# Plain float32 products in four column groups for the first modulation, and the first products in feature order

## The chip, the cores and the metric

The kernel runs on one core of a Trainium2 chip. The metric is the device time of one execution in microseconds. Engines are named as in the profile: PE is TensorE (PEld its weight loads), DVE VectorE, ACT ScalarE, POOL GpSimd, SP the engine whose queue issues nearly all DMA transfers.

## The reference

One layer of a diffusion backbone: 1024 latent tokens and 256 context tokens of width 1024. The part at issue is its start: a conditioning vector gives shifts and scales (a vector-matrix product with `w_mod`), these modulate an RMS norm, and the result goes through the input projection.

```python
sc, scc = jax.nn.silu(c), jax.nn.silu(c_ctx)
m_lat = sc @ w_mod[l] + b_mod[l]
m_ctx = scc @ w_mod[l] + b_mod[l]
sh1, sc1, g1, sh2, sc2, g2 = [t[:, None, :] for t in jnp.split(m_lat, N_MOD, axis=-1)]
csh1, csc1, cg1, csh2, csc2, cg2 = jnp.split(m_ctx, N_MOD, axis=-1)

h_lat = rms_norm(x, norm1_g[l]) * (1.0 + sc1) + sh1
h_ctx = rms_norm(ctx, norm1_g[l]) * (1.0 + csc1) + csh1
...
split_heads(h_lat @ w_in, rope_r, rope_d)
split_heads(h_ctx @ w_in, None, None)
...
k_all = jnp.concatenate([dk_c, dk_l], axis=3)
```

Retention, differential attention, output projection, gated residual, a second modulated norm, a gated MLP with a depthwise convolution, and a final norm follow; the change touches none of them.

## The kernel before

Everything is in float32. A large product is made of three passes over operands split into a high and a low float32r part (helper `passes`, L129 to L132: high x high, high x low, low x high), each a 128 x 128 weight block against up to 512 columns. Plain float32 products are used in a few places.

**Start of the kernel.** Four blocks of `w_mod`, 512 columns wide (1024 x 512, the order of the blocks is scale and shift of features 0 to 511, then scale and shift of features 512 to 1023), are loaded as 16 tiles `wt` of 512 KB, two blocks of 128 rows each. `modulation1(half)` does two of the blocks. For each 128-row block the silu of the two conditioning vectors (`csil`, 128 x 2) is the weight of a matmul and the `wt` rows stream past: into `pr`, one PSUM bank. The string table `GEMV` says which of the 32 row blocks go as a plain float32 product (L506, "1", 21 of them) and which as a split one (L511 to L514, "0", 11 of them): ACT makes `mhi`, DVE makes `mlo`, and two float32r matmuls with `csplit` (4 columns: high and low part of both vectors) take them. At the end of a block ACT copies `pr` to `rw`, and four short products with `fold` (L520), called a fold below, add the parts up and turn the row into columns `mcol`, to which DVE adds the bias. So there are four folds, two in each half.

**Beside it.** `raw_latents` loads the first four tiles `xt` of 128 tokens, normalizes them (ACT squares, DVE, POOL's power step, DVE multiplies, L529 to L531) and turns them with PE transposes `px` into `xraw` (features on partitions). `xt` and `wt` share one ring of five 512 KB buffers, so each transfer waits until the one five places ahead is used up. After the second fold `first_latents(0)` modulates features 0 to 511 (L582 on DVE, high part L583 on ACT, low part L585 on DVE or POOL) and does their part of the products for the attention's keys: heads `h` outside, feature blocks `k` inside, three passes each into `pl`. It is called by `tick` from inside the modulation's loop, so its steps stand between the weight products of the second half. The w_in slices `raw` that these products need are split into `whi` and `wlo` by `split_slice` (L180 to L184). After the fourth fold comes the rest: features 512 to 1023 of the same products and `rotated` (rotary step and store), with `context_rows` beside it (two tiles `xc`, turned and modulated into `cT`), then the products `pc` of the context, with the second four token tiles (`latents`) beside them, then `pl` of the second token half, 96 products, then the value projection `pn`.

**What sets the order.** The program order is written by hand with `beside` and `tick`. A scheduler then lists the instructions per engine by its own cost model and buffer counts; each engine runs its list in order. Each transfer of SP's queue waits in line too.

## Time and profile before

| | |
|---|---|
| median of 3 runs | 1462.45 us (1458.42 to 1463.15) |
| profiled execution | 1465.94 us, its span 1464.2 us |
| mean granted TensorE clock | 0.990 |
| PE busy in 0 to 32 us | 24.13 us |
| DVE busy in 60 to 80 us | 19.04 us |
| `wt` transfers | 16 of 512 KB, median 4.4 us from issue to landing |

The span runs from the first to the last instruction. Times in the views are from the span's start. A timeline row gives the start, the time from the first start to the last end of the merged instructions, the engine, the line, the names and the count, and in brackets the idle time before it and what ended that. Matmuls are pipelined: a record's length is more than the step to the next one.

### The profile page before, as it was taken

The page shows a single profiled execution, that of the slowest core. Times are in us where ns is not written, and L with a number is a line of the kernel's source. Part 1 is how long each engine was busy: PE and PEld are TensorE (multiplying, and loading weights), DVE is VectorE, ACT ScalarE, POOL GpSimd, SP SyncE. Part 2 cuts the span into 40 slices and gives each one's busy share as a digit, 9 for nine tenths or more (in the row PEclk, how much of TensorE's full clock was granted, in tenths as well). Part 3 has the DMA queues.
Part 4 walks back from the last instruction along what each step waited for, and adds up shares of the span by engine and source line. Part 5 has one row for each costly group of instructions (what it writes and reads, how often), then busy time and mean ns, then how long its engine had stood idle before and what let it go on. Part 6 is the DMA issues. An engine that isn't in the chain of part 4 may idle for free.

```text
span 1464.2 us, 19441 instructions
## 1 busy us (share of the span) xinstructions
PE 1399.3 (96%) x6924; PEld 1145.3 (78%) x6924; DVE 1008.7 (69%) x1491; ACT 739.6 (51%) x1409; POOL 362.7 (25%) x466
## 2 busy tenths in 40 slices
PE   7999999999899899889999989999999999999996
PEld 2587888787778789779888767888888888888885
DVE  4687355333577599778334889777787787998457
ACT  4665212322456688778423654555544545555433
POOL 1320000021788324651001253222322220000001
PEclk9999999999999999999999999999999999999999
DMA  8548755465455757561322123222332234963324
GB/s 289 204 169 274 241 180 174 142 188 180 140 168 174 192 126 183 137 119 30 141 104 87 43 94 123 93 96 106 108 109 104 98 108 148 387 220 115 101 94 173
DMA packets 107753, 218.30 MB, mean 149 GB/s; under 512 B 8964, under 2 KB 47364, under 8 KB 106760
## 3 DMA queue, kind: packets, MB, share of 16 engines
q1 hardware_dynamic: 99592, 192.41, 38.6%
q0 software_dynamic: 8064, 24.64, 7.4%
q8 instruction: 55, 0.90, 0.3%
q14 instruction: 42, 0.34, 0.1%
HBM read 159.61 MB, written 57.41 MB: 148 GB/s over the span
## 4 chain that ended last, share of the span: by engine, by line
PE 69%; DVE 8%; DMA 6%; ACT 4%; POOL 3%; issue 3%; SPq 0%; POOLq 0%; DVEq 0%; ACTq 0%
PE chain L130 5%; PE chain L131 5%; PE chain L132 5%; PE pv L774 4%; PE pA L742 4%; PE c L132 3%; PE c L131 3%; PE c L130 3%; PE pn L130 3%; PE pn L132 3%; PE pn L131 3%; PE third L130 2%; DMA W<-w_down 2%; PE third L132 2%; PE third L131 2%
## 5 line engine op out<-in xcount | busy, mean ns | idle before, releaser
L130 PE MATMUL pl<-hT,whi 128*128 128x512 f32 x256 | 107.6, 422 | 0.7 <-ACT hT L583 0.7
L130 PE MATMUL chain<-T,whi 128*128 128x512 f32 x264 | 103.5, 392 | 3.1 <-ACT ub L1120 1.3
L131 PE MATMUL pl<-hT,whi 128*128 128x512 f32 x256 | 101.8, 398 | 1.6 <-DVE hT L585 1.3
L131 PE MATMUL chain<-T,whi 128*128 128x512 f32 x264 | 102.9, 390 | 0.0
L132 PE MATMUL chain<-T,wlo 128*128 128x512 f32 x264 | 102.3, 390 | 0.4 <-DVE wlo L909 0.4
L132 PE MATMUL pl<-hT,wlo 128*128 128x512 f32 x256 | 101.0, 395 | 0.5 <-DVE wlo L184 0.5
L742 PE MATMUL pA<-ks,qhl 128*128 128x512 f32 (+1 forms) x384 | 94.3, 383 | 4.5 <-ACT p L749 4.5
L745 DVE TENSOR_REDUCE mt<-pA 128x1 f32<-128x1280 f32 x64 | 95.1, 1488 | 3.7 <-PE pA L742 2.3
L1036 POOL TENSOR_TENSOR cmb<-wrb 128x512 f32<-128x512 f32 x22 | 35.3, 1603 | 247.8 <-DMA wrb<-w_up 138.6
L132 PE MATMUL c<-whi,ghl 128*128 128x512 f32 x232 | 90.4, 390 | 0.3 <-DVE ghl L1195 0.3
L130 PE MATMUL c<-whi,ghl 128*128 128x512 f32 x232 | 90.3, 389 | 0.0
L131 PE MATMUL c<-wlo,ghl 128*128 128x512 f32 x232 | 90.3, 389 | 0.0
L749 ACT ACTIVATE p<-pA,mt 128x1280 f32<-128x1280 f32 x64 | 85.3, 1332 | 5.0 <-DVE mt L745 4.9
L116 POOL TENSOR_TENSOR sm<-sm,mhalf 128x1 f32<-128x1 f32 x26 | 16.7, 640 | 283.1 <-DVE sm L115 277.2
L742 PEld LDWEIGHTS pA<-ks,qhl 128*128 128x128 f32 x384 | 71.0, 198 | 17.7 <-ACT p L749 5.5
L908 ACT CAST whi<-cmb 128x512 fp32r<-128x512 f32 x66 | 41.0, 622 | 83.2 <-PE chain L131 61.2
L909 DVE TENSOR_TENSOR wlo<-cmb,whi 128x512 fp32r<-128x512 f32 x66 | 63.7, 968 | 23.4 <-ACT whi L908 23.3
L774 PE MATMUL pv<-va,aT 128*128 128x128 f32 x640 | 77.8, 277 | 0.5 <-DVE yT L803 0.2
L130 PE MATMUL pn<-whi,hT 128*128 128x512 f32 x192 | 77.8, 405 | 0.0
L774 PEld LDWEIGHTS pv<-va,aT 128*128 128x128 f32 x640 | 73.9, 192 | 2.7 <-DVE yT L803 1.9
L132 PE MATMUL pn<-whi,hT 128*128 128x512 f32 x192 | 75.4, 393 | 0.0
L131 PE MATMUL pn<-wlo,hT 128*128 128x512 f32 x192 | 75.1, 391 | 0.0
(309 smaller groups left out, 3934.1 us busy)
## 6 DMA issues: line engine op xcount, KB each, us to landing
wm<-w_mod SPq DMA_DIRECT2D x32, 512.0 KB, 4.5
raw<-w_in SPq DMA_DIRECT2D x28, 512.0 KB, 4.5
wra<-w_up SPq DMA_DIRECT2D x24, 512.0 KB, 3.3
wrb<-w_up SPq DMA_DIRECT2D x24, 512.0 KB, 3.4
W<-w_down SPq DMA_DIRECT2D x44, 256.0 KB, 6.2
ad<-s SPq DMA_DIRECT2D x20, 512.0 KB, 3.3
wra<-ad SPq DMA_DIRECT2D x20, 512.0 KB, 3.3
wrb<-ad SPq DMA_DIRECT2D x18, 512.0 KB, 3.4
```

Of the source, the lines that this page charges most:

```text
L116: nc.gpsimd.tensor_tensor(out=out_ap, in0=out_ap, in1=mhalf[:, :n], op=ALU.pow)
L130: mm(ps, lh, rh, start=first, stop=False, skip_group_check=more)
L131: mm(ps, lh, rl, start=False, stop=False, skip_group_check=more)
L132: mm(ps, ll, rh, start=False, stop=last, skip_group_check=more)
L742: mm(self.pa[m][:, c0:c1], self.q[:, i, m, qs], self.k[:, m, c0:c1], start=(i == 0), stop=(i == 1))
L745: nc.vector.tensor_reduce(out=self.mt[:, m : m + 1], in_=self.pa[m][:, :LK], axis=AX.X, op=ALU.min)
L749: nc.scalar.activation(self.p[m], self.pa[m][:, :LK], AF.Exp, scale=-1.0, bias=self.mt[:, m : m + 1], accum_out=self.s[:, m : m + 1])
L774: mm(self.pv, self.aT[:, c, :], self.v[:, c, :], start=(c == 0), stop=(c == NKT - 1))
L908: nc.scalar.copy(hi, src)
L909: nc.vector.tensor_tensor(out=lo, in0=src, in1=r32(hi), op=ALU.subtract)
L1036: nc.gpsimd.tensor_tensor(out=s1, in0=b1, in1=b2, op=ALU.add)
```

## The change

The table `GEMV` and the split path are gone: all 32 row blocks go as plain float32 products. `cz` holds the two conditioning columns with 30 zero columns behind them for each row block (a POOL memset and a DVE copy). Four row blocks at a time, each with its own 32 columns as weights, write the partitions 0 to 31, 32 to 63, 64 to 95 and 96 to 127 of `pr`; a second group of four adds to them. `fold` is now 128 x 2 and adds up the four groups. `rw` is 128 rows high instead of 4.

The order around it changes too. The loads of the four `x` tiles are issued from inside the modulation, one before every second `wt` tile; a token tile is turned one step later than it is normalized; the two w_in slices that were loaded in the first half come behind all of its loads. The products of features 0 to 511 run in feature order: block `k` outside, the four heads inside, with all four `pl` banks open. The rest of the features runs heads 0 and 1 together in feature order, then head 2, then head 3.

```diff
--- before.py
+++ after.py
@@ -58,7 +58,6 @@
 R_LAM = R_DEC + 8
 
 
-GEMV = ("01111111", "00111111", "01010101", "01010101")
 TAIL = 2
 EARLY = ("S1", "M1", "S0", "M0", "E1", "E0", "R", "C")
 OPS = dict(S="scores", M="least", E="exp", R="ratio", C="combine", T="turn", K="turned", V="values", O="out", Q="square", f="rstd", n="norm", Y="final", h="high", l="low")
@@ -485,36 +484,34 @@
 
         with ExitStack() as p0:
             xp = p0.enter_context(tc.tile_pool(name="xp", bufs=1))
-            csplit = xp.tile([P, KD, 4], F32R, name="csplit")
-            nc.vector.tensor_copy(csplit[:, :, 0:2], csil)
-            nc.vector.tensor_tensor(out=csplit[:, :, 2:4], in0=csil, in1=r32(csplit[:, :, 0:2]), op=ALU.subtract)
-            fold = xp.tile([4, 2], F32, name="fold")
-            nc.vector.tensor_tensor(out=fold, in0=ident[:4, 0:2], in1=ident[:4, 2:4], op=ALU.add)
-            bsc = xp.tile([P, KD], F32, name="bsc", bufs=3)
+            cz = xp.tile([P, KD, 32], F32, name="cz")
+            nc.gpsimd.memset(cz, 0.0)
+            nc.vector.tensor_copy(cz[:, :, 0:2], csil)
+            fold = xp.tile([P, 2], F32, name="fold")
+            nc.vector.tensor_tensor(out=fold, in0=ident[:, 0:2], in1=ident[:, 32:34], op=ALU.add)
+            for g in (64, 96):
+                nc.vector.tensor_tensor(out=fold, in0=fold, in1=ident[:, g : g + 2], op=ALU.add)
+            bsc = xp.tile([P, KD], F32, name="bsc", bufs=7)
             nc.vector.tensor_scalar(out=bsc, in0=cl[:, COL_BMOD + 8 : COL_BMOD + 16], scalar1=1.0, scalar2=None, op0=ALU.add)
 
-            def modulation1(half):
+            def modulation1(half, between, beyond):
+
                 d0 = 4 * half
                 for i in range(2 * half, 2 * half + 2):
                     s = 1 - i % 2
                     pr = mm_tile("pr")
-                    for kk in range(KD // 2):
-                        raw = xp.tile([P, 2, 512], F32, name="wt", tag="xt", bufs=5)
-                        nc.sync.dma_start(out=raw, in_=w_mod[i][:, 2 * kk : 2 * kk + 2, :])
-                        for j in range(2):
-                            if GEMV[i][2 * kk + j] == "1":
-                                mm(pr[:2, :], csil[:, 2 * kk + j, :], raw[:, j, :], start=False, stop=(kk + j == KD // 2))
-                                tick()
-                                continue
-                            whi = xp.tile([P, 512], F32R, name="mhi", bufs=2)
-                            wlo = xp.tile([P, 512], F32R, name="mlo", bufs=2)
-                            nc.scalar.copy(whi, raw[:, j, :])
-                            nc.vector.tensor_tensor(out=wlo, in0=raw[:, j, :], in1=r32(whi), op=ALU.subtract)
-                            mm(pr[:4, :], csplit[:, 2 * kk + j, :], whi, start=(kk + j == 0), stop=False)
-                            mm(pr[:4, :], csplit[:, 2 * kk + j, :], wlo, start=False, stop=(kk + j == KD // 2))
-                            tick()
-                    rw = xp.tile([4, 512], F32, name="rw", bufs=2)
-                    nc.scalar.copy(rw, pr[:4, :])
+                    for q in range(2):
+                        raw = []
+                        for kk in (2 * q, 2 * q + 1):
+                            raw.append(xp.tile([P, 2, 512], F32, name="wt", tag="xt", bufs=5))
+                            nc.sync.dma_start(out=raw[-1], in_=w_mod[i][:, 2 * kk : 2 * kk + 2, :])
+                            if kk % 2 == 0:
+                                next(between, None)
+                        for g in range(4):
+                            mm(pr[32 * g : 32 * g + 32, :], cz[:, 4 * q + g, :], raw[g // 2][:, g % 2, :], start=(q == 0), stop=(q == 1))
+                        next(beyond, None)
+                    rw = xp.tile([P, 512], F32, name="rw", bufs=2)
+                    nc.scalar.copy(rw, pr)
                     pm = pst.tile([P, 4, 2], F32, name="pm", tag="tr")
                     for j in range(4):
                         mm(pm[:, j, :], rw[:, j * P : (j + 1) * P], fold, start=True, stop=True)
@@ -558,39 +555,61 @@
             wget, more = stream_parts(5)
             part = []
 
+            xs0 = []
+
+            def row_loads():
+                for t in range(4):
+                    xs0.append(xp.tile([P, D], F32, name="xt", tag="xt", bufs=5))
+                    nc.sync.dma_start(out=xs0[t], in_=x[t * P : (t + 1) * P, :])
+                    yield
+
+            def turn_raw(t):
+                for g in range(2):
+                    pt = pst.tile([P, 4, P], F32, name="px", tag="tr")
+                    for i in range(4):
+                        d = 4 * g + i
+                        nc.tensor.transpose(pt[:, i, :], xs0[t][:, d * P : (d + 1) * P], ident)
+                    dst = xraw[:, 4 * g : 4 * g + 4, t * P : (t + 1) * P]
+                    if g == 0:
+                        nc.scalar.copy(dst, pt)
+                    else:
+                        nc.vector.tensor_copy(dst, pt)
+
             def raw_latents():
                 for t in range(4):
-                    xt = xp.tile([P, D], F32, name="xt", tag="xt", bufs=5)
-                    nc.sync.dma_start(out=xt, in_=x[t * P : (t + 1) * P, :])
+                    normalize(xs0[t], 2 + t)
+                    if t:
+                        turn_raw(t - 1)
                     yield
-                    normalize(xt, 2 + t)
-                    for g in range(2):
-                        yield
-                        pt = pst.tile([P, 4, P], F32, name="px", tag="tr")
-                        for i in range(4):
-                            d = 4 * g + i
-                            nc.tensor.transpose(pt[:, i, :], xt[:, d * P : (d + 1) * P], ident)
-                        dst = xraw[:, 4 * g : 4 * g + 4, t * P : (t + 1) * P]
-                        if g == 0:
-                            nc.scalar.copy(dst, pt)
-                        else:
-                            nc.vector.tensor_copy(dst, pt)
-
-            def first_latents(half):
-                for d in range(4 * half, 4 * half + 4):
-                    hi, lo, raw = hT[0][0][:, d, :], hT[1][0][:, d, :], xraw[:, d, :]
-                    nc.vector.tensor_scalar(out=raw, in0=raw, scalar1=mcol[:, d, 1, 0:1], scalar2=mcol[:, d, 0, 0:1], op0=ALU.mult, op1=ALU.add)
-                    nc.scalar.copy(hi, raw)
-                    eng = nc.gpsimd if d % 2 else nc.vector
-                    eng.tensor_tensor(out=lo, in0=raw, in1=r32(hi), op=ALU.subtract)
+
+            def modulated(d):
+                hi, lo, raw = hT[0][0][:, d, :], hT[1][0][:, d, :], xraw[:, d, :]
+                nc.vector.tensor_scalar(out=raw, in0=raw, scalar1=mcol[:, d, 1, 0:1], scalar2=mcol[:, d, 0, 0:1], op0=ALU.mult, op1=ALU.add)
+                nc.scalar.copy(hi, raw)
+                eng = nc.gpsimd if d % 2 else nc.vector
+                eng.tensor_tensor(out=lo, in0=raw, in1=r32(hi), op=ALU.subtract)
+
+            def part_products(h, k):
+                passes(part[h], wget(k, h * P, (h + 1) * P), tuple(hT[a][0][:, k, :] for a in range(2)), k == 0, k == KD - 1)
+
+            def first_half():
+                part.extend(mm_tile("pl") for _ in range(H))
+                for k in range(4):
+                    modulated(k)
+                for k in range(4):
+                    for h in range(H):
+                        part_products(h, k)
                     yield
-                for h in range(H):
-                    if half == 0:
-                        part.append(mm_tile("pl"))
-                    for k in range(4 * half, 4 * half + 4):
-                        passes(part[h], wget(k, h * P, (h + 1) * P), tuple(hT[a][0][:, k, :] for a in range(2)), k == 0, k == KD - 1)
-                        yield
-                    if half == 1:
+
+            def second_half():
+                for k in range(4, KD):
+                    modulated(k)
+                for hs in ((0, 1), (2,), (3,)):
+                    for k in range(4, KD):
+                        for h in hs:
+                            part_products(h, k)
+                            yield
+                    for h in hs:
                         rotated(part[h], dk_d, rtab, 32, 1.0, LC, h, 0)
 
             def context_rows():
@@ -608,19 +627,16 @@
                     modulate(xc, d, 1, cT[0][:, d, :], cT[1][:, d, :])
                     yield
 
-            beside(raw_latents(), 0.75, 1.0)
-            modulation1(0)
+            modulation1(0, row_loads(), raw_latents())
+            turn_raw(3)
             more()
             more()
-            beside(first_latents(0), 1.25, 0.0)
-            modulation1(1)
-            beside(iter(()), 0.0)
+            modulation1(1, iter(()), first_half())
             more()
             more()
             rtab = load_rope(1)
-            todo = first_latents(1)
-            for _ in range(4):
-                next(todo)
+            todo = second_half()
+            next(todo)
             beside(context_rows(), 0.75, 0.0)
             for _ in todo:
                 tick()
```

Three places of the built order show what this moves. First PE from the start of the modulation to the second fold; `pr` are the weight products, `px` the turns of the token tiles, `pm` a fold. Before:

```order
L513 MATMUL pr<-mhi,csplit 4x512
L514 MATMUL pr<-mlo,csplit 4x512
L506 MATMUL pr<-wt,csil 2x512 x2
L572 MATMUL px<-ident,xt 128x128 x4
L506 MATMUL pr<-wt,csil 2x512
L572 MATMUL px<-ident,xt 128x128 x4
L506 MATMUL pr<-wt,csil 2x512 x3
L572 MATMUL px<-ident,xt 128x128 x4
L506 MATMUL pr<-wt,csil 2x512
L572 MATMUL px<-ident,xt 128x128 x4
L520 MATMUL pm<-fold,rw 128x2 x4
```

Now:

```order
L511 MATMUL pr<-wt,cz 32x512 x4
L571 MATMUL px<-ident,xt 128x128 x8
L511 MATMUL pr<-wt,cz 32x512 x4
L517 MATMUL pm<-fold,rw 128x2 x4
L571 MATMUL px<-ident,xt 128x128 x7
L511 MATMUL pr<-wt,cz 32x512 x2
L571 MATMUL px<-ident,xt 128x128
L511 MATMUL pr<-wt,cz 32x512 x2
L571 MATMUL px<-ident,xt 128x128 x8
L511 MATMUL pr<-wt,cz 32x512 x4
L517 MATMUL pm<-fold,rw 128x2 x4
L571 MATMUL px<-ident,xt 128x128 x8
```

The first list ends at the first fold, the second at the turns of the last token tile, behind the second fold: the weight products stand in runs of two tiles, and the turns of a token tile are no longer spread between them.

SP's queue over the same stretch. Before:

```order
L503 DMA wt<-w_mod 128x1024
L564 DMA xt<-x 128x1024
L503 DMA wt<-w_mod 128x1024
L564 DMA xt<-x 128x1024
L503 DMA wt<-w_mod 128x1024 x2
L180 DMA raw<-w_in 128x1024
L564 DMA xt<-x 128x1024
L503 DMA wt<-w_mod 128x1024 x2
L564 DMA xt<-x 128x1024
L503 DMA wt<-w_mod 128x1024 x2
L180 DMA raw<-w_in 128x1024
L503 DMA wt<-w_mod 128x1024 x8
```

Now:

```order
L507 DMA wt<-w_mod 128x1024
L563 DMA xt<-x 128x1024
L507 DMA wt<-w_mod 128x1024 x2
L563 DMA xt<-x 128x1024
L507 DMA wt<-w_mod 128x1024 x2
L563 DMA xt<-x 128x1024
L507 DMA wt<-w_mod 128x1024 x2
L563 DMA xt<-x 128x1024
L507 DMA wt<-w_mod 128x1024
L179 DMA raw<-w_in 128x1024 x2
L507 DMA wt<-w_mod 128x1024 x8
```

The two w_in slices have moved behind the last transfer of the first half; a token tile now comes with every two weight tiles.

DVE around the fourth fold, which ends in the row `mcol<-pm,cl`; `xc` are the context tiles. Before:

```order
L184 TENSOR_TENSOR wlo<-raw,whi 128x1024 x2
L512 TENSOR_TENSOR mlo<-wt,mhi 128x512
L115 TENSOR_SCALAR sm<-sm 128x1
L531 TENSOR_SCALAR xc_540<-xc_540,sm 128x1024
L115 TENSOR_SCALAR sm<-sm 128x1
L531 TENSOR_SCALAR xc_550<-xc_550,sm 128x1024
L523 TENSOR_TENSOR mcol<-pm,cl 128x4x2
L115 TENSOR_SCALAR sm<-sm 128x1
L582 TENSOR_SCALAR xraw<-xraw,mcol 128x512 x4
L585 TENSOR_TENSOR hT_170<-xraw,hT_168 128x512
```

Now:

```order
L183 TENSOR_TENSOR wlo<-raw,whi 128x1024
L520 TENSOR_TENSOR mcol<-pm,cl 128x4x2
L587 TENSOR_SCALAR xraw<-xraw,mcol 128x512
L183 TENSOR_TENSOR wlo<-raw,whi 128x1024
L590 TENSOR_TENSOR hT_170<-xraw,hT_168 128x512
L587 TENSOR_SCALAR xraw<-xraw,mcol 128x512 x3
L590 TENSOR_TENSOR hT_170<-xraw,hT_168 128x512
L114 TENSOR_SCALAR sm<-sm 128x1
L528 TENSOR_SCALAR xc_490<-xc_490,sm 128x1024
L114 TENSOR_SCALAR sm<-sm 128x1
L528 TENSOR_SCALAR xc_500<-xc_500,sm 128x1024
```

The context tiles are normalized behind the modulation of the second four feature blocks, where they stood ahead of the fourth fold, and one of two splits of a w_in slice has moved behind the fold.

## The prediction

> **What bounds the kernel now.** I read the page first (busy shares, then the 40 slices), then the table of stretches, then the timeline of the first 130 us. The built order of every engine differs only there and in a few places up to about 180 us; behind that it is the same instruction for instruction.
>
> ```profile
> PE 1399.3 (96%) x6924; PEld 1145.3 (78%) x6924; DVE 1008.7 (69%) x1491; ACT 739.6 (51%) x1409; POOL 362.7 (25%) x466
> ...
> sum 32.00, PE 24.13 PEld 7.92 DVE 12.13 ACT 14.16 POOL 2.39; mean PE 1.51 PEld 0.49 DVE 0.76 ACT 0.89 POOL 0.15
> ...
> 20.00:25.00 5.00, 4.71 (x14) 1.55 (x14) 1.65 (x6) 1.74 (x3) 0.55 (x1) 0.66 0.86 302
> ...
> 60.00:65.00 5.00, 3.36 (x11) 1.89 (x12) 4.77 (x6) 2.81 (x7) 3.70 (x3) 1.00 0.00 0
> 65.00:70.00 5.00, 5.00 (x24) 4.03 (x24) 4.53 (x9) 4.89 (x10) 1.74 (x3) 1.00 0.01 3
> 70.00:80.00 10.00, 9.36 (x62) 7.89 (x61) 9.74 (x19) 9.71 (x18) 2.99 (x3) 1.00 0.19 73
> ```
>
> TensorE is busy 96% of the span, so a microsecond taken off it early moves everything behind. In a row of the table the columns are PE, PEld, DVE, ACT, POOL, then the clock. TensorE is also what the first 32 us wait for (24.13 busy, and nearly all of its idle time is before the first weights arrive), then up to 58 us. From 60 to 80 us VectorE is full (4.77, 4.53 and 9.74, 19.04 of 20 us) and TensorE has holes. So there are three stages with different limits: first half of the modulation (to the second fold), second half (to the fourth fold), and a tail that VectorE sets.
>
> ```profile
> 5.85 0.62 ACT L511 CAST mhi<-wt 128x512 fp32r<-128x512 f32 x1 [2.83 <-DMA wt<-w_mod]
> 7.10 1.06 ACT L529 ACTIVATE sq<-xt 128x1024 bf16<-128x1024 f32 x1 [0.63 <-DMA xt<-x]
> 7.77 3.25 PE L506 MATMUL pr<-wt,csil 128*2 128x512 f32 x4
> 8.58 0.13 PEld L506 LDWEIGHTS pr<-wt,csil 128*2 128x2 f32 x1 [0.72 <-DMA wt<-w_mod]
> 9.68 1.06 ACT L529 ACTIVATE sq<-xt 128x1024 bf16<-128x1024 f32 x1 [1.43 <-DMA xt<-x]
> 13.08 2.74 PE L506 MATMUL pr<-wt,csil 128*2 128x512 f32 x6
> 28.20 0.66 PE L572 MATMUL px<-ident,xt 128*128 128x128 f32 x4
> 29.84 0.58 ACT L517 COPY rw<-pr 4x512 f32<-4x512 f32 x1 [0.36 <-PE pr L506]
> 30.47 1.05 PE L520 MATMUL pm<-fold,rw 4*128 4x2 f32 x8
> 31.45 0.40 PE L513 MATMUL pr<-mhi,csplit 128*4 128x512 f32 x1
> ...
> L506 PE MATMUL pr<-wt,csil x42: 591/592/1061, 7.8 to 55.4; 128*2 128x512 f32 x42
> ...
> wt<-w_mod SPq DMA_DIRECT2D x16, 512.0 KB, 4.4
> ```
>
> A plain float32 product is two records (x42 for 21 products). Six take 2.74 us and the last is 0.592 long, so the pitch is (2.74 - 0.59)/5 = 0.43 us, 0.86 for a product. Early ones ran at nearly twice that (four in 3.25). The second fold ends at 31.45, the fourth, below, at 58.50.
>
> **The change, part by part.** It removes 21 plain products, 11 split ones (22 short matmuls, with 11 copies on ACT and 11 subtractions on DVE) and adds 32 plain products, four to a group, each in its own 32 columns. DVE and ACT were not the limit before 58 us, so their savings there count for nothing; what counts is the price of a group on TensorE.
>
> That price no row shows: nothing in this trace runs in another column group. Bounds from the 0.43 pitch: the records of a pair one after the other, 4 x 0.43 = 1.72; both products wholly at once, 2 x 0.43 = 0.86. Between them: the low record of one product must follow its own high record, but the next product's high record can run beside it, 3 x 0.43 = 1.29 (five pitches, 2.15, for four). I take this middle, since matmuls here start in program order, and keep both ends. [...]
>
> *First half.* Here the loads set the pace. The first five 512 KB transfers (five buffers) land at 5.85, 7.10, 8.58, 9.68 and, by the same step of 1.25, about 11.0. The new order takes w0 w1, turns x0, takes w2 w3, folds, turns x1, takes w4 w5, turns x2, takes w6 w7, folds, turns x3. The w0 w1 products at the slow early pitch end about 10.5; eight turns (2 x 0.66) 11.8; w2 and w3 (asked for when w0 is free, about 8.7, landed by 12.9) 14.1; copy 0.58 and fold 1.05 to 15.8; turns of x1 to 17.1. Only that frees the buffer of w6. The queue is in order, so w6 lands some 4 us later at 21.2 (median 4.4), x3 at 22.4, w7 at 23.7; their products to 25.0, copy and fold to 26.6. So the second fold ends 31.45 - 26.6 = 4.9 earlier. Serial products make it 28.8 (2.7 earlier), wholly parallel ones 26.0 (5.5 earlier). TensorE now waits on loads from 18 to 23, and where it paused before, the granted clock fell (0.66 in 20 to 25); a repeat would cost up to 2 of this.
>
> *Second half.*
>
> ```profile
> 30.43 0.69 DVE L577 COPY xraw<-px 128x512 f32<-128x512 f32 x1 [1.59 <-PE px L572]
> 32.25 1.00 DVE L582 TENSOR_SCALAR xraw<-xraw,mcol 128x512 f32<-128x512 f32 x2
> 32.88 1.14 ACT L583 CAST hT<-xraw 128x512 fp32r<-128x512 f32 x2 [1.42 <-DVE xraw L582]
> 50.04 0.40 PE L130 MATMUL pl<-hT,whi 128*128 128x512 f32 x1
> 50.27 0.39 PE L131 MATMUL pl<-hT,whi 128*128 128x512 f32 x1
> 54.99 1.02 PE L506 MATMUL pr<-wt,csil 128*2 128x512 f32 x2
> 55.94 0.50 PE L130 MATMUL pl<-hT,whi 128*128 128x512 f32 x1
> 57.52 1.05 PE L520 MATMUL pm<-fold,rw 4*128 4x2 f32 x8
> 58.50 0.64 PEld L537 LDWEIGHTS pt<-ident,xc 128*128 128x128 f32 x6
> ```
>
> Before, 58.50 - 31.45 = 27.05. A feature product has a pitch of 0.23; entering and leaving a plain product costs 55.94 - 54.99 - 0.86 = 0.09. Now: the eight turns of x3 (1.32), the copy (0.69), the modulation of one feature block (0.50) and its high part (0.57) come first, 3.1; then 48 feature products x 0.23 = 11.0, six pairs of weight products x 1.38 = 8.3, one run of four 2.24, two folds x 0.98 = 2.0. Sum 26.6, a gain of 0.4. Serial: eight x 1.81 = 14.5 in place of 10.5, 30.6, a loss of 3.6. Parallel: seven entries x 0.95 = 6.7, 22.8, a gain of 4.3. The w_in slices, which now queue behind all the first half's loads, land about 26, before their use at 28.
>
> Fourth fold: 4.9 + 0.4 = 5.3 earlier; serial 0.9 later, parallel 9.8 earlier.
>
> *Tail.*
>
> ```profile
> 60.61 3.55 POOL L585 TENSOR_TENSOR hT<-xraw,hT 128x512 fp32r<-128x512 f32 x2 [0.76 <-ACT hT L583]
> 65.44 0.75 DVE L531 TENSOR_SCALAR xt<-xt,sm 128x1024 f32<-128x1024 f32 x1 [0.66 <-POOL sm L116]
> 92.61 0.40 PE L130 MATMUL pl<-hT,whi 128*128 128x512 f32 x1
> 95.52 0.68 DVE L544 TENSOR_TENSOR hT<-tmp,hT 128x512 fp32r<-128x512 f32 x1
> 115.00:120.00 5.00, 3.02 (x13) 1.87 (x12) 5.00 (x7) 4.56 (x8) 0.00 (x0) 1.00 0.82 273
> 120.00:125.00 5.00, 3.82 (x17) 2.83 (x16) 4.55 (x6) 1.20 (x2) 0.00 (x0) 1.00 1.00 344
> 126.01 1.22 DVE L184 TENSOR_TENSOR wlo<-raw,whi 128x1024 fp32r<-128x1024 f32 x1
> ...
> PE pn L131 <- DVE wlo L184: 1.9, 1, 1.9
> ```
>
> Both context tiles were normalized before the fourth fold. Now that stands behind the second features' modulation on DVE, and its power step behind POOL's low parts, 3.55 for two; one wlo split (1.22) also slips behind the fold, another moves ahead of the second token half. That is 2 x (0.75 + 0.15) + 2 x 1.22 = 4.2 more on the engine that is full there, and a wait for POOL. Walking the new order with these durations, the last low part on DVE comes 45 after the fourth fold, where it was at 96.2 - 58.5 = 37.7. TensorE can do 33 of the 96 products of the second token half by then and ends them 59.8 after the fold, not 92.61 + 96 x 0.23 - 58.5 = 56.3: 3.4 lost. But it then runs into a wait it has already: 1.98 + 1.18 = 3.2 idle from 115 to 125, until the fourth split of the value weights, done 127.2 - 58.5 = 68.7 after the fold. In the new order I get 66.8, because VectorE's idle gaps behind 96 us are used up. The wait that ends last decides: between 1.9 gained and, if it is gone, 3.4 lost. I take 1.0 gained.
>
> *Sum:* 4.9 + 0.4 + 1.0 = 6.3 us. The profiled execution took 1465.94 (span 1464.2), 3.5 above the median of the runs, so 1459.6 against it and 1462.45 - 6.3 = 1456.2 against the median.
>
> **Rivals.**
>
> *Columns wholly at once.* 9.8 + 1.0 = 10.8 gained, 1451.7. For: four groups have four destinations and the source lays them next to each other. Against: each product is two records that need the same columns. [...]
>
> *Columns one after another.* 0.9 lost, 1.0 gained in the tail: 1462.3, no change. For: every plain record in this trace follows the one before at a full pitch. Against: all those share their columns, so they had to.
>
> *Every step between column groups exposes a weight load.* This is the other side. Place: second half, where nothing covers TensorE.
>
> ```profile
> 11.54 0.09 PEld L506 LDWEIGHTS pr<-wt,csil 128*2 128x2 f32 x2 [0.17 <-issue]
> 13.51 0.08 PEld L506 LDWEIGHTS pr<-wt,csil 128*2 128x2 f32 x1 [0.34 <-issue]
> ```
>
> Price: on top of serial products, the 0.17 seen where kinds change, on 32 records, 5.4, and about 1 more in the first half: 0.9 + 5.4 + 1.0 - 1.0 = 6.3 lost, 1468.8. It decides (slower by over 0.3%) from about 0.12 a record. Against: the load at 13.51 ran inside the matmul before. [...]
>
> *The tail's lag goes through.* 45 - 37.7 = 7.3 lost instead of 1.0 gained: 5.3 - 7.3 = 2.0 slower, 1464.5. For: VectorE is full from 60 to 80. Against: TensorE has 33 products and all context products to do meanwhile.
>
> **How the numbers follow.** About 0.3% (4.4 us) is what a measurement of this kernel can tell from no change. The forecast (partial overlap) has 0.38: of it 0.28 faster, 0.09 within, 0.01 slower; own range 1452 to 1460. Wholly parallel 0.22, all faster. Serial 0.18: 0.03 faster, 0.11 within, 0.04 slower. Exposed loads 0.13, slower. Tail 0.09: 0.03, 0.04, 0.02. Together 0.56, 0.24 and 0.20. The range runs from 1449 (past the parallel case) to 1467 (short of exposed loads).
>
> **What would show it.** The starts of the eight records of a group: steps of 0, 0.43, 0, 0.43 between products mean partial overlap, all within 0.86 parallel, eight even steps serial; wider ones exposed loads. The second fold should end near 26.6 and the fourth near 53.2. In the tail, the last low part of the second token half some 45 after that, and a TensorE wait before the value products that ends about 67 after it. A second fold later than 29, or a group that takes over 3.4, makes the forecast wrong.

## The result, and the profile after

The changed kernel took 1463.25 us (median of 22 runs, 1459.24 to 1469.08), the kernel before 1462.37 us beside it (22 runs, 1458.42 to 1467.4). The ratio is 1.0002, with a 95% interval from 0.999 to 1.0014: no change that can be told. Forecast were 1456.2 us and, as the likeliest, faster.

The profiled execution of the changed kernel has a span of 1458.7 us, 5.5 below that of the kernel before. That difference is not the change. The last value product on context tiles (behind the work that the change touches) starts at 244.15 us, before at 243.49; the 5.5 us arise later, in work that both kernels share. There the trace of the kernel before has four more stretches at half the clock than that of the changed one (from about 260, 365, 510 and 600 us), each worth 1.7 us of clock. The table of stretches shows the first of them. First the kernel before, then the changed one; the number ahead of the last two is the granted clock:

```profile
255.00:260.00 5.00, 2.52 (x9) 1.43 (x9) 4.59 (x6) 0.98 (x2) 0.00 (x0) 0.97 0.42 157
260.00:265.00 5.00, 5.00 (x17) 3.37 (x16) 0.69 (x1) 1.76 (x3) 0.00 (x0) 0.68 0.50 184
```

```profile
255.00:260.00 5.00, 3.32 (x12) 1.99 (x11) 4.58 (x7) 1.29 (x3) 0.00 (x0) 1.00 0.42 151
260.00:265.00 5.00, 5.00 (x26) 3.97 (x25) 0.56 (x1) 1.55 (x3) 0.00 (x0) 1.00 0.51 185
```

A hole here is a time in which TensorE stands. Both traces have one (5 - 2.52 = 2.5 us and 5 - 3.32 = 1.7); one was followed by a stretch at half the clock (17 matmuls in 5 us instead of 26), the other was not. So a single trace says little of the whole time here, and I compare milestones of the first 250 us.

The same table of the changed kernel for the first 90 us (PE, PEld, DVE, ACT, POOL, then the clock):

```profile
15.00:20.00 5.00, 2.99 (x16) 0.92 (x15) 1.78 (x5) 1.74 (x3) 0.55 (x1) 1.00 0.90 335
20.00:25.00 5.00, 3.06 (x17) 1.08 (x17) 1.60 (x3) 2.32 (x4) 0.55 (x1) 1.00 1.01 382
25.00:30.00 5.00, 3.11 (x17) 2.71 (x17) 2.09 (x4) 2.27 (x4) 0.00 (x0) 0.57 1.01 385
30.00:35.00 5.00, 5.00 (x12) 1.85 (x14) 4.71 (x7) 2.48 (x4) 1.72 (x2) 0.50 0.43 137
35.00:40.00 5.00, 5.00 (x19) 1.99 (x18) 0.15 (x1) 0.00 (x0) 1.27 (x1) 0.91 0.51 164
55.00:60.00 5.00, 4.76 (x13) 3.64 (x14) 4.20 (x7) 3.39 (x7) 2.54 (x2) 0.66 0.51 178
80.00:90.00 10.00, 6.97 (x50) 5.53 (x49) 8.07 (x15) 6.72 (x12) 3.42 (x4) 1.00 0.45 159
```

TensorE now has holes from 15 to 30 us (it waits for the modulation's weights, for the copies of its own results and for the token tiles), and the clock is at half from 25 to 35 us and again between 56 and 60. The clock lost is (0.43 + 0.50 + 0.09) x 5 = 5.1 us, and 0.34 x 5 = 1.7 more; the kernel before had one such stretch here, 1.7 us. (This counts clock, not time: where TensorE stands anyway, a low clock costs nothing.) From 80 to 90 us TensorE stands 3 of 10 us. The timeline of TensorE shows what the low clock does, and the price of the column groups (L511 their products, L571 the turns, L517 the folds, L129 to L131 the products of the first features):

```profile
24.97 1.26 PE L517 MATMUL pm<-fold,rw 128*128 128x2 f32 x8 [0.69 <-ACT rw L514]
26.09 1.95 PE L571 MATMUL px<-ident,xt 128*128 128x128 f32 x8
31.07 1.92 PE L511 MATMUL pr<-wt,cz 128*32 128x512 f32 x4
...
45.25 1.05 PE L511 MATMUL pr<-wt,cz 128*32 128x512 f32 x4
46.23 0.50 PE L130 MATMUL pl<-hT,whi 128*128 128x512 f32 x1
...
48.95 1.07 PE L511 MATMUL pr<-wt,cz 128*32 128x512 f32 x8
49.94 0.50 PE L129 MATMUL pl<-hT,whi 128*128 128x512 f32 x1
52.80 0.95 PE L517 MATMUL pm<-fold,rw 128*128 128x2 f32 x8
55.24 0.97 PE L129 MATMUL pl<-hT,whi 128*128 128x512 f32 x3 [1.49 <-ACT hT L588]
```

A pair of products takes 46.23 - 45.25 = 0.98 us, four take 49.94 - 48.95 = 0.99: the columns run wholly at once. A pair takes 1.92 at half clock. (The pair at 8.21 us takes 1.92 too, where the clock column reads 1.00; what slows it there is not shown.) The second fold ends at 26.2 and the fourth at 53.75, 4.75 us earlier than before.

The tail is the work from the fourth fold to the first value product on latents (`pn` from `hT`). First two rows and a stretch of the kernel before:

```profile
68.75 1.06 ACT L529 ACTIVATE sq<-xt 128x1024 bf16<-128x1024 f32 x1
127.09 0.39 PE L130 MATMUL pn<-whi,hT 128*128 128x512 f32 x1
...
80.00:90.00 10.00, 9.26 (x73) 8.35 (x71) 8.85 (x15) 8.22 (x13) 2.40 (x2) 1.00 0.40 152
```

The changed kernel, in rows of ScalarE, VectorE and TensorE and of TensorE's waits:

```profile
65.42 4.82 ACT L420 ACTIVATE xb<-pl 32x512 f32<-32x512 f32 x8
82.38 1.05 ACT L526 ACTIVATE sq<-xt 128x1024 bf16<-128x1024 f32 x1
87.06 0.55 PE L534 MATMUL pt<-ident,xt 128*128 128x128 f32 x3 [1.32 <-DVE xt L528]
99.62 0.68 DVE L541 TENSOR_TENSOR hT<-tmp,hT 128x512 fp32r<-128x512 f32 x1
116.15 0.39 PE L131 MATMUL pl<-hT,wlo 128*128 128x512 f32 x1
123.78 1.21 DVE L183 TENSOR_TENSOR wlo<-raw,whi 128x1024 fp32r<-128x1024 f32 x1
128.57 0.39 PE L129 MATMUL pn<-whi,hT 128*128 128x512 f32 x1
...
PE pt L534 <- DVE xt L528: 2.2, 2, 1.3
```

The first value product on latents starts at 128.57 us, 74.8 after the fourth fold, where it was 127.09 - 58.50 = 68.6: 6.2 us lost, against 4.75 gained ahead of it.

### The profile page after: what moved, and what is told of

Same layout as the page of the kernel before. It is cut to its first block, busy times and chain, and to the rows that moved or that the text cites. A ratio compares the mean times of both kernels' runs of the same rounds, so it can differ in the third digit from the quotient of the medians.

```text
span 1458.7 us, 19406 instructions
## 1 busy us (share of the span) xinstructions
PE 1388.4 (95%) x6924; PEld 1142.0 (78%) x6924; DVE 995.8 (68%) x1481; ACT 732.6 (50%) x1398; POOL 360.6 (25%) x467
## 4 chain that ended last, share of the span: by engine, by line
PE 69%; DVE 10%; DMA 8%; ACT 5%; POOL 4%; issue 4%; SPq 0%; POOLq 0%; ACTq 0%; DVEq 0%
PE chain L129 5%; PE chain L130 5%; PE chain L131 5%; PE pv L790 4%; PE c L131 3%; PE c L129 3%; PE c L130 3%; PE pA L758 3%; PE pn L130 3%; PE pn L131 3%; PE pn L129 3%; PE third L129 2%; PE third L130 2%; PE third L131 2%; PE po L131 2%
## 5 line engine op out<-in xcount | busy, mean ns | idle before, releaser
L129 PE MATMUL pl<-hT,whi 128*128 128x512 f32 x256 | 108.1, 426 | 4.0 <-ACT hT L588 3.4
L129 PE MATMUL chain<-T,whi 128*128 128x512 f32 x264 | 103.5, 392 | 3.0 <-ACT ub L1136 1.3
L131 PE MATMUL chain<-T,wlo 128*128 128x512 f32 x264 | 102.4, 390 | 0.4 <-DVE wlo L925 0.4
L131 PE MATMUL pl<-hT,wlo 128*128 128x512 f32 x256 | 102.0, 399 | 0.0
L131 PE MATMUL c<-whi,ghl 128*128 128x512 f32 x232 | 90.4, 389 | 0.5 <-DVE ghl L1211 0.5
L129 PE MATMUL c<-whi,ghl 128*128 128x512 f32 x232 | 90.3, 389 | 0.0
L129 PE MATMUL pn<-whi,hT 128*128 128x512 f32 x192 | 78.2, 407 | 0.0
L131 PE MATMUL pn<-whi,hT 128*128 128x512 f32 x192 | 75.0, 391 | 0.0
```

The lines of the kernel that those rows point to most:

```text
L129: mm(ps, lh, rh, start=first, stop=False, skip_group_check=more)
L131: mm(ps, ll, rh, start=False, stop=last, skip_group_check=more)
```

## The experiments

Three theories of where the gain went were tried. **Clock**: the faster columns leave TensorE waiting, the granted clock halves behind such holes, and that takes the gain. **Tail**: two heads now end together, their rotation copies fill ScalarE (65.42, 4.82 us), the normalizations of the second token half come late (squares to 83.4 us, before to 70), and TensorE has holes from 80 to 101 us. **Order**: computing the first features' products in feature order is what costs. A table of all runs first. Clock is the mean over the timed runs of each kernel (in brackets: one run). The last three columns, in us, are from one trace each: end of the fourth fold, start of the first value product on latents, start of the last value product on context tiles. A filler is a product whose result nothing reads.

| kernel | ratio to before (95%) | clock | fold | latents | context |
|---|---|---|---|---|---|
| before | 1 | 0.991 | 58.5 | 127.1 | 243.5 |
| changed | 1.0002 (0.999 to 1.0014) | 0.987 | 53.8 | 128.6 | 244.2 |
| e5, changed again | one run | (0.990) | 53.0 | 127.7 | 242.7 |
| e1, early normalization | 1.0007 (0.9992 to 1.0022) | 0.9865 | 54.5 | 129.1 | 247.1 |
| e2, head order | 1.0016 (1.0005 to 1.0027) | 0.985 | 52.0 | 127.1 | 243.4 |
| e3, 48 fillers | 0.9964 (0.9949 to 0.9978) | 0.9915 | 52.8 | 126.3 | 242.2 |
| e4, one column set | one run | (0.991) | 59.6 | 128.0 | 242.6 |
| e6, 25 fillers | 0.9969 (0.9955 to 0.9983) | 0.992 | 48.1 | 121.7 | 237.6 |
| e7, fillers, head order | 0.999 (0.9977 to 1.0003) | 0.991 | 49.3 | 122.4 | 238.6 |
| e8, e7 with early norm. | 0.9998 (0.9981 to 1.0014) | 0.991 | 48.1 | 121.2 | 238.2 |
| e9, e6, early norm., own raw | 0.9984 (0.9966 to 1.0001) | 0.991 | 49.9 | 119.9 | 241.7 |
| e10, e6, own raw | 0.9982 (0.997 to 0.9994) | 0.991 | 48.6 | 121.5 | 240.5 |
| e11, 19 fillers | one run | (0.991) | 48.1 | 121.6 | 237.5 |
| e12, before with 3 fillers | one run | (0.991) | 58.0 | 126.0 | 244.2 |

**Four products through one set of columns (e4).**

```
-mm(pr[32 * g : 32 * g + 32, :], ..., start=(q == 0), stop=(q == 1))
+mm(pr[:32, :], ..., start=(q + g == 0), stop=(q + g == 4))
```

> The changed kernel with all four weight tiles of a run put through the same 32 columns, added up in one place, so that nothing can run side by side; same count of products, fold over 32 rows instead of 128. If the groups of the changed kernel run wholly at once (run of four 0.99 us, one alone 0.86): a run of four takes 3.3 to 3.5 us here, second fold later by 1 to 4 us (loads cover part), fourth fold later by 9 to 12 us than 53.75, span 5 to 12 us longer. If the columns gave nothing and the pace came from elsewhere: a run of four stays below 1.5 us and the folds within 1 us.

From its timeline and its table of stretches:

```profile
52.09 3.62 PE L509 MATMUL pr<-wt,cz 128*32 128x512 f32 x8
58.58 1.05 PE L515 MATMUL pm<-fold,rw 32*128 32x2 f32 x8
...
20.00:25.00 5.00, 3.56 (x20) 1.79 (x19) 2.64 (x4) 2.81 (x6) 0.55 (x1) 1.00 1.02 389
25.00:30.00 5.00, 4.33 (x14) 1.19 (x12) 2.18 (x4) 2.58 (x4) 0.55 (x1) 1.00 0.88 274
```

Four products in one place take 3.62 us, beside each other 1.07 in the same measure: 3.4 times. But the fourth fold is only 5.9 us later than in the changed kernel (9 to 12 expected), and nothing runs at half speed: the clock is 1.00 up to 260 us. And at 128 us the two kernels stand together (128.0 against 128.6). The comparison at full clock is with e6 below, the changed kernel with its holes filled: there the fold is 59.6 - 48.1 = 11.5 us earlier than here, as expected, the first value product on latents 6.3, the last on context tiles 5.0. The eight weight loads of a run of four are 0.109 us each (median of the changed kernel), 0.87 us one after another; in the run at 48.95 us of the changed kernel they lie within 0.16 us at its start, so they run beside each other too.

**Fillers for the clock (e3, e6, e11).** They are products of the ones tile with itself, 128x128, and each run of them stands behind a chosen product (the lines that fix its place are not shown):

```
+def warm(n):
+    wm = pst.tile([P, P], F32, name="wm", tag="tr")
+    ...
+    for _ in range(n):
+        mm(wm, ones, ones, start=True, stop=True)
 for g in range(4):
+    if i == 1 and g == 2:
+        warm(4 if q == 0 else 5)
     mm(pr[32 * g : 32 * g + 32, :], ...)
 turn_raw(3)
+warm(8)
```

These lines are of e6, which has 2 more ahead of the second fold and 6 behind the fourth; e11 leaves the 6 out. In e3 they stand in runs of 8, 8, 8, 12 and 12.

> The changed kernel with short products of the ones tile (128x128, results never read) put into the waits of TensorE: eight behind each of three quarters of the first half, twelve ahead of the second half's columns, twelve behind the fourth fold. They compute nothing that is used. Clock theory: the granted clock stays near 1.0 from 25 to 35 us (0.57 and 0.50 in the changed kernel), the stretch from the first features' products to the second pair of columns takes 3.4 instead of 6.4 us, and the fourth fold ends at 49.5 to 51.5 instead of 53.75. If loads bind instead: clock near 1.0 but the fold within 1 us of 53.75. If the clock follows something other than the idle of TensorE: 0.5 to 0.6 stays. For the whole time: tail theory says that an earlier fold is lost again behind late normalizations, ratio 0.999 to 1.001; if the tail passes it on, 0.997 to 0.998.

The clock stayed up but for one stretch at 27 to 30 us (mean of the timed runs 0.9915, changed kernel 0.987), and the time fell by 0.36%, more than expected for an earlier fold. The fillers were too many: they pushed the second fold from 26.2 to 31.8 us, and the fourth, at 52.8, missed its forecast (49.5 to 51.5) but still came 0.95 earlier than in the changed kernel. At the last value product on context tiles only 243.5 - 242.2 = 1.3 us are gained on the kernel before; where the rest of the 0.36% arises is not shown.

> The changed kernel with 25 short products of the ones tile (results never read) fitted into the holes of TensorE that its trace shows: 4 and 5 between the two products of the third and fourth runs of the first half, 2 ahead of the second fold, 8 behind the last turns, 6 behind the fourth fold; in all 6.0 us of work at 0.24 us each (from the run with 48 of them), 6.7 us of holes. Clock theory: no half-speed period ahead of 60 us (6.8 us lost in the changed kernel), second fold at 25 to 26.5, fourth fold at 48.5 to 50.5 instead of 53.75, time 1456 to 1459, ratio 0.996 to 0.998, spread of the runs smaller. If only the tail's order counts: fold earlier, last value product on context tiles still at 243 to 244.5, ratio 0.999 to 1.001.

Its timeline and table:

```profile
21.05 1.05 PE L522 MATMUL pr<-wt,cz 128*32 128x512 f32 x4 [0.25 <-DMA wt<-w_mod]
22.03 1.38 PE L501 MATMUL wm<-ones 128*128 128x128 f32 x10
26.11 0.95 PE L530 MATMUL pm<-fold,rw 128*128 128x2 f32 x8
47.17 0.95 PE L530 MATMUL pm<-fold,rw 128*128 128x2 f32 x8
121.72 0.39 PE L129 MATMUL pn<-whi,hT 128*128 128x512 f32 x1
...
25.00:30.00 5.00, 5.00 (x48) 4.75 (x50) 3.51 (x6) 3.46 (x5) 0.00 (x0) 1.00 0.99 385
30.00:35.00 5.00, 4.16 (x24) 2.33 (x20) 4.41 (x7) 2.29 (x4) 1.82 (x2) 1.00 0.86 304
55.00:60.00 5.00, 4.90 (x25) 3.76 (x26) 3.03 (x8) 2.99 (x6) 1.89 (x3) 1.00 0.05 20
```

The second fold ends at 27.1 (25 to 26.5 forecast), 0.8 later than in the changed kernel, the clock is 1.00 up to 60 us, and the fourth fold ends at 48.1 us, 5.6 earlier. All of it is still there at 122 us (121.7 against 128.6) and at 238. The time is 1457.09 us, median of 7 runs, against 1463.12 beside it (25 runs). Its ratio lies, like that of e3, below those of both kernels with intervals apart, by work that computes nothing.

> The changed kernel with the 19 short products of the first half and last turns, and without the 6 behind the fourth fold. Clock theory: no half-speed period from 25 to 35 us, fourth fold at 47.5 to 48.5 (53.75 in the changed kernel), then one period of half speed begins within 5 us of the fold's end (1.5 us of hole there, as in both traces of the changed kernel), and first value product on latents at 122.5 to 124, that is 1 to 2 us behind the run with all 25. If the six are worthless: within 0.5 us of 121.7.

No half-speed stretch followed the hole behind the fourth fold here (1.49 us), and the six were worth nothing in this trace (121.6 us): the second branch. So the same hole is followed by half speed in both traces of the changed kernel and not in this one. The traces together say more than one of them. The four with columns and without fillers (changed, e5, e1, e2) have three or more half-speed stretches from 20 to 60 us each; the six with the fitted fillers (e6 to e11) have none there.

**A second trace of the changed kernel (e5).**

> The changed kernel itself, nothing edited, for a second trace. Clock theory (runs of the changed kernel hold a mean granted clock of 0.987 against 0.991 of the kernel before, though the one trace at hand has 0.991; the clock is lost in whole periods of 3.4 us at half speed that follow a period with holes on TensorE, and which periods are hit differs from run to run): the half-speed periods ahead of 60 us come again, and this trace shows 1 to 4 further ones, above all between 80 and 130 us, where the first trace has holes. Tail theory alone: the same periods as in the first trace, the same span within 1 us.

```profile
20.00:25.00 5.00, 4.48 (x18) 2.09 (x20) 1.00 (x3) 1.63 (x3) 0.40 (x1) 0.66 0.97 334
30.00:35.00 5.00, 4.73 (x14) 1.79 (x14) 4.71 (x7) 2.83 (x5) 1.30 (x2) 0.66 0.76 279
55.00:60.00 5.00, 5.00 (x16) 3.79 (x15) 3.39 (x6) 3.98 (x8) 3.35 (x3) 0.66 0.38 135
```

Three stretches ahead of 60 us, 5.1 us of clock, at other places than in the first trace; none between 80 and 130 us, where I expected more. (Such ones do come in the traces of e2, at 85 to 95 us, and e1, at 120.)

**The tail (e1, e2).** In e1 the loads and normalizations of xc and of x4 to x7 are called right behind the second half's modulation; in e2 both halves take the products head by head.

```
 next(todo)
+rows_of(xc, ctxt, NTC, "xc{}", 0)
+rows_of(xs, x[4 * P : 8 * P, :], 4, "xt", 6, tag="xt", bufs=5)
```

> The changed kernel with one edit: the two context tiles and latent tiles x4 to x7 are loaded and normalized in program order right behind the fourth fold's modulation, ahead of the products of the second half and of the rotations of their heads; no arithmetic differs. Late-normalization theory (the tail loses about 5 us because the squares of x5 to x7 stand behind the rotations' copies on ScalarE, 78.8 to 83.4 us, so the turns of the second token half wait): the squares come by about 65 us, the stop-and-go of TensorE between 80 and 101 us goes, first value product on latents at 123 to 125 instead of 128.6, last value product on context tiles (243.7) 3 to 5 us earlier, time about 1458 to 1460, ratio 0.997 to 0.998. Rival, the order of the first features' products costs the tail by itself: milestones stay within 1 us of the changed kernel's, ratio 0.9995 to 1.001. Rival, the half clock at 55 to 60 us is what is lost: the same, no change at 128.6 beyond 1 us.

> The changed kernel with the products of the first features put back head by head in both halves (as in the kernel before), the column groups and the loads left as changed. Order theory (feature order finishes two heads together, so their rotations' eight copies block ScalarE from 65.4 to 70.2 us and push everything behind): tail recovers 3 to 5 us, first value product on latents at 124 to 126, ratio about 0.997. Late-normalization theory with the loads as its cause: rotations come one head at a time, but the squares of x5 to x7 stay late; first value product on latents within 1.5 us of 128.6, ratio 0.999 to 1.001.

In e1 the squares are done by 69.6 us and the first value product on context comes at 113.53 instead of 116.38. Then this row of TensorE's timeline:

```profile
120.76 0.79 PE L129 MATMUL pn<-whi,cT 128*128 128x512 f32 x1 [2.76 <-ACT whi L182]
```

It waits 2.76 us for the last slice of the value weights, and the clock halves behind that (0.66 from 120 to 125 us). The first value product on latents comes at 129.1, the last on context tiles 2.9 us later than in the changed kernel, and the time is that of the kernel before. None of the figures forecast for the tail theory came; the ratio is the one forecast for its rivals, but the milestones moved (2.9 us earlier at 113 us, 2.9 later at 247), so normalizing early does act, and the later wait takes what it gains. In e2 the first value product on latents recovers 1.5 us of the 3 to 5 forecast for the order theory, the last on context tiles 0.8, the squares still end at 81.3 us, and the time is 0.14% above the changed kernel's, with intervals that overlap (and 0.16% above the kernel before, clear of it): head order is no cure.

**Both cures together (e7, e8).**

> The run with fitted products, and the products of the first features head by head (the edit of the run on head order). There the span multiplied by the granted clock was the lowest (1441.7 against 1442.8 for the changed kernel and 1447.4 for the kernel before), but the clock too (0.985). Clock theory: with the clock held to 60 us the head order keeps its advantage, 1454 to 1458, ratio 0.994 to 0.997. Order theory in its other form (head order is slower whatever the clock): ratio at least 0.002 above that of the run with fitted products alone.

> As the run before, and the context and latent tiles loaded and normalized early (the edit of the first run). If early normalization only moved the wait to the split of the value weights (there TensorE stood 2.2 us at 118 us and the clock halved behind it): ratio within 0.0015 of the run with fitted products and head order. If its gain was hidden by clock falls: ratio 0.001 to 0.003 below that run.

The time hoped for did not come: 0.999 and 0.9998. For e7 that is the second branch, by a hair (0.0021 above e6); but its interval overlaps with that of e6, so that head order is slower is not shown. For e8 it is the first (0.0008 above e7). Up to 239 us the traces stand within 1.2 us of that of e6 at the three milestones.

**The value weights' last slice in a buffer of its own (e9, e10).** It shared two raw buffers with the slices ahead of it.

```
-wg = stream_block(6)
+wg = stream_block(6, m2p)
 ...
-raw = wr.tile([P, 2, 512], F32, name="raw")
+raw = (pool or wr).tile([P, 2, 512], F32, name="raw")
```

> Fitted products, early load and normalization of the context and latent tiles (products of the first features in the changed kernel's order), and a raw buffer of its own for the last slice of the value weights, so that its load need not wait until an earlier slice is split. Theory that the value weights absorb what the tail gains (first value product 2 to 3 us earlier with early normalization in two runs, then TensorE waits 1.9 and 2.8 us for the last slice): the wait is under 0.5 us here, first value product on latents at 117.5 to 119.5 (121.7 in the run with fitted products), last value product on context tiles 233.5 to 236 (237.6), time 1452 to 1456, ratio 0.993 to 0.996. If the slice's wait is a matter of ScalarE and VectorE rather than of its load: 120.5 or later, ratio within 0.001 of the run with fitted products (0.9969).

> Fitted products and the raw buffer of its own for the last slice of the value weights, without early normalization. There the wait at that slice was 0.7 us in all, so both theories give little: first value product on latents 121 to 122, ratio 0.996 to 0.9975. Together with the run before it prices early normalization with the absorber gone.

In e9 the wait for the slice is gone, so it was one for the raw buffer, and the first value product on latents comes at 119.9, 1.8 us ahead of e6 (117.5 to 119.5 forecast). Then its timeline of VectorE and TensorE has:

```profile
132.35 1.29 DVE L463 SCALAR_TENSOR_TENSOR macc<-wm,csil,macc 128x1024 f32<-128x1024 f32 x1
133.74 2.89 PE L468 MATMUL pg<-macc,ones 128*128 128x512 f32 x4 [3.21 <-issue]
```

The gate's modulation (macc, eight loads of weights multiplied and added on VectorE) ends at 133.6; TensorE has nothing before it in its order and stands 3.21 us, then runs at 0.70 of the clock (135 to 140 us). In e6 it stood 1.26 us there. In e10 it stands 2.85 us there. The last value product on context tiles is 4 us later in e9 than in e6, where it was forecast 1.5 to 4 earlier. Both times miss their forecasts and read above that of e6, with intervals that overlap.

**The kernel before with three fillers (e12).**

> The kernel before with three short products of the ones tile ahead of its first fold, where its trace has a hole of 0.64 us and a half-speed period behind it (20.9 to 24.3 us). Clock theory: that period is gone, second fold ends 1 to 2 us ahead of 31.45, fourth fold 1 to 2 us ahead of 58.5; no more is to be had, as the kernel before has no other half-speed period until 255 us. If the fall at 20.9 us has another cause: it stays.

The stretch at 21 to 24 us is gone, but the second and fourth fold come only 0.55 us earlier (1 to 2 forecast), and by 244 us nothing is left. So in this one run the fillers do little where there was one half-speed stretch; it is the changed kernel that gains by them.

## Why the prediction failed

*What failed.* Two steps: the tail, put at 1.0 gained, and the clock, put at nothing in the sum. Where the first value product on latents starts, 6.3 us were to be gained and 127.09 - 128.57 = -1.5 were. The fourth fold took its share of that almost as forecast (4.75 for 5.3), and the tail lost 6.2 in place of gaining 1.0.

*Price of a group.* I took partial overlap (pair 1.38 us with entering and leaving, four 2.24) and gave the columns at once 0.22. Measured were 0.98 and 0.99. In the run of four at 48.95 us the first records of all four products start within 0.02 us, the second ones from 49.40 on: a second record comes 0.45 behind its own first, as assumed, but no product waits for another. (The profile has two records for a product and does not say what each holds; high and low are the prediction's names.) The step was mis-sized on the safe side: with the clock held, the fourth fold ends at 48.1 us (e6), 10.4 earlier than before; forecast were 5.3, and 9.8 for the rival that was right. The sum for serial products holds too: 0.9 later was forecast for the fourth fold, and e4 has it 1.1 later.

*Clock.* The prediction saw that the clock may fall again and wrote that a repeat "would cost up to 2", outside the sum. Filling the holes moves the fourth fold by 53.75 - 48.1 = 5.6 us (e6). So the fold at 53.75, where 53.2 was forecast, is luck: columns that were 5 us better and a clock that was 5 us worse. In clock, the two traces lost 6.8 and 5.1 us ahead of 60 us, the kernel before 1.7. The timed runs agree in size: (1 - 0.987) x 1461.7 = 19.0 us of clock lost in the changed kernel, (1 - 0.9905) x 1461.3 = 13.9 in the kernel before, 5.1 apart. They don't say where in the kernel, and the two traces of the changed kernel come from runs with a higher clock than most (0.991 and 0.990 against a mean of 0.987). The removal of the holes (e3, e6) brings the mean clock back to 0.992 and the median time to 3.5 and 6.0 us below the kernel before.

*Tail.* "1.0 gained" was wrong, in sign too. The last low part on VectorE came 100.3 - 53.75 = 46.5 after the fold (forecast 45). But the products of the second token half end at 116.5 - 53.75 = 62.8, not 59.8; and the fourth split of the value weights ends at 125.0 - 53.75 = 71.2, not 66.8. I took that wait for a fixed date into which a late TensorE could run for nothing. It is none: the slice's load stands in SP's queue until the split of an earlier slice has freed the raw buffer (0.6 us in this trace, 2.5 in that of e1), and a buffer of its own takes that wait away (e9). That the splits are late because the products ahead of them release their buffers late is argued from the source, not shown. With the clock held the tail loses 121.7 - 48.1 - 68.6 = 5.0 us.

*The sum.* Forecast 5.3 + 1.0 = 6.3 gained. Measured in the traces: 10.4 from the change at full clock, 5.6 lost to the clock, 6.2 lost in the tail. They cancel to what was measured, no change. That e6 comes within 1 us of the forecast 1456.2 is an accident of sizes.

*Rivals.* Exposed weight loads did not come (the eight of a run of four lie within 0.16 us). The tail's lag (0.09) was right that the tail loses: its 7.3 stand against 6.2 in the trace, and 5.0 with the clock held. It named a full VectorE as the reason; here the late squares on ScalarE stand at the start of the lag, and e1, which moves them ahead, gains 2.9 us up to 113 us. Feature order by itself is not the cause (e2, e7).

*What stays open.* Why e7 to e10, level with e6 or nearly so at 122 us, end 3 to 5 us behind it by the medians (2 to 4 by the ratios, with intervals that overlap or nearly so). For e9 and e10 part of it is the gate's wait; for e7 and e8 their traces show half-speed stretches at 255 and 365 us where that of e6 has only the second, but those move from run to run. Early normalization gains at 113 us and nothing at the end; the waits that take it are shown (value weights, then the gate), but their removal one by one was not carried to an end.

## What to carry to other kernels

A faster form of a matmul in a stage that waits for loads makes holes, and here their price was less their length than the half clock that followed (with them filled the fourth fold came 5.6 us earlier, e6): look for the holes of the new schedule, and fill them, or spend them on work that is needed. How full is full enough was not measured. Check a saved microsecond against each later wait in turn: here the value weights (a wait of 2.76 us in e1), then the gate's modulation (3.21 in e9), took what early normalization saved ahead of them. Where runs scatter by 3 us and the effect is 5, read milestones close behind the change and the mean clock of all runs, not one trace's span.

## What was not expected of the hardware

In this trace the clock falls in whole stretches of 3.4 us. Slices of 1 us of the changed kernel (length, PE busy, clock, DMA share, GB/s):

```profile
22.00:23.00 1.00, 0.00 (x0) 1.00 1.00 344
...
25.00:26.00 1.00, 1.00 (x8) 0.83 1.02 410
...
35.00:36.00 1.00, 1.00 (x5) 0.55 0.71 291
36.00:37.00 1.00, 1.00 (x5) 1.00 0.00 0
...
55.00:56.00 1.00, 0.76 (x3) 1.00 0.86 352
56.00:57.00 1.00, 1.00 (x4) 0.69 0.43 86
...
59.00:60.00 1.00, 1.00 (x4) 0.61 0.00 0
60.00:61.00 1.00, 1.00 (x6) 1.00 0.00 0
```

From the shares of the slices: half speed from 25.7 to 35.9 us by this reading, 10.2 us or three times 3.4, and from 56.4 to 59.8, 3.4. In the 8 us ahead of the first no hole was longer than 1.4 us (the one at 22 us is 1.25), and ahead of the second stands the one of 1.49. The same hole of 1.49 us in e11 has no half speed behind it: there the clock is 1.00 up to 250 us. What decides where a stretch begins is not shown.

The two records of a plain float32 product, which followed each other 0.43 us apart in the kernel before, run beside those of three other products when each has its own 32 columns: four cost what two cost (0.99 and 0.98 us).
